# Seven block products instead of eight for three of eight k-tile pairs of the gate and up products

## The chip, the cores and the metric

The kernel runs on one core of a Trainium2 chip. The time is the device time of one execution in microseconds (us); a comparison takes the median of several runs. The profile is one execution taken by the hardware profiler. TensorE is called PE, with its weight loads apart as PEld, VectorE is DVE, ScalarE is ACT, GpSimd is POOL; SP is the queue that issues nearly all DMAs.

## The reference

One layer of a streaming encoder, 256 tokens of 2048 channels, all in float32:

```
x = x + 0.5 * swiglu(rms_norm(x, ffn1_norm), w_gate, w_up, w_down)
h = rms_norm(x, mix_norm);  proj = h @ w_in
x = x + concat([pool_mixer(u), gla_mixer(q, k, v, g, a)]) @ w_out
x = x + mem_cross_attention(rms_norm(x), rms_norm(mem), w_q, w_kv, w_o)
x = x + 0.5 * swiglu(rms_norm(x, ffn2_norm), w_gate, w_up, w_down)
out = rms_norm(x, final_norm)

def swiglu(h, w_gate, w_up, w_down):
    return (silu(h @ w_gate) * (h @ w_up)) @ w_down      # 2048 -> 5632 -> 2048
```

The change concerns `h @ w_gate` and `h @ w_up` in both feed-forward parts.

## The kernel before

**Numbers.** A float32 product is made of three products of float32r parts. An activation or a weight `a` is split into `hi` (a cast on ACT) and `lo = a - hi` (a subtraction on DVE); the product is `hi*hi + hi*lo + lo*hi`, three matmuls (`products`, L277). `xs` and `ys` hold activations already split, 16 k-tiles of 128 channels, each with hi and lo and 256 tokens, that is two halves of 128 tokens.

**Units.** All weights pass through one stream of units (`Stream`, L34). A unit is 1 MB of weights, 128 x 2048 float32. SP loads it into one of three `raw` buffers, ACT casts it into `wh` and DVE makes `wl` (three buffers each), and PE uses it. `emit` (L65) writes the program in this order: the split of unit u+2, the load of unit u+5, the matmuls of unit u. Work beside the stream (evictions, transposes, norms) is put in with `st.op(f, n)`: n units later. A scheduler at build time may still move instructions within an engine's list, but each engine then works its list strictly in order.

**Gate and up.** For 1024 output columns a `block_t` (L284) runs eight units over the 16 k-tiles, two k-tiles a unit. With two k-tiles, two column halves j and two token halves h a unit has eight block products of 128 x 128 by 128 x 512, 24 matmuls. They gather in two PSUM tiles of two banks each; PSUM holds four such tiles. The gate block is evicted by ACT (`ev_gate`, L463: Silu), the up block by DVE (`ev_up`, L468: times the gate), and the result is transposed by PE into `ys` (`turn`, L476: 16 transposes for a pair of blocks, then a cast and a subtraction for each half).

The loop (L486) goes over three parts of the 5632 columns: 4, 4 and 3 column blocks of 512. A part is two, two or one pairs of a gate and an up block (the third part ends with a block that holds 512 columns of both), and is followed by its down product (`into_x`, or `down_end` at the very end), whose units are plain ones too. A feed-forward part has 132 units; both have ten gate or up blocks of full width, five of each.

Of the kernel before, what the change touches and what calls it, by code (L numbers as in the profile page):

```python
# [33 lines left out]
class Stream:  # L34
# [23 lines left out]

    def unit(self, load, f, split=None):
        self.items.append((len(self.units), f))  # L60
        self.units.append((load, split))
        self.pending = [(n - 1, h) for n, h in self.pending]
        self._flush()

    def emit(self, load, split):  # L65
        done, w = -1, {}
# [12 lines left out]

def build(ctx, tc, I, out):  # L80
# [35 lines left out]
    def ctile():  # L116
        return tmp.tile([P, 2, S], F32, tag="c", name=uid("c"), bufs=2)

    def ttile():
        return tmp.tile([P, 2, S], F32, tag="t", name=uid("t"), bufs=3)  # L120

# [17 lines left out]


    ident = head.tile([P, 480], F32, tag="ident", name="ident")[:, :P]
    make_identity(nc, ident)
# [3 lines left out]
    for t in range(PAD):  # L146
        nc.gpsimd.memset(invc[:, t : t + 1], 1.0 / (t + 1))
    keep = const.tile([P, S], F32, tag="keep", name="keep")
    nc.gpsimd.memset(keep, 1.0)
    for c in range(S // CH):  # L150
        nc.gpsimd.memset(keep[:, c * CH : c * CH + 1], 0.0)
    gains = ctl("gains", [P, G_END])
    wa2 = const.tile([32, H * DK], F32, tag="wa2", name="wa2")
    R = const.tile([P, S], F32, tag="R", name="R")
    Rcol = ctl("Rcol", [P, 2])
# [36 lines left out]
    def diagonal(col):  # L192
        d = tmp.tile([P, P], F32, tag="diag", name=uid("diag"), bufs=4)
        nc.vector.tensor_scalar_mul(d, ident, col)
        return d
# [25 lines left out]

    diag = {}

# [7 lines left out]
    def spread_norm():  # L231

        ps = ptile(uid("ps"))
        for t in range(2):
            spread(ps[:, 0, :], t, diag["R"][t])
        nc.vector.tensor_copy(R, ps[:, 0, :S])

# [46 lines left out]
    def block_t(srcs, act, evict, delays=(0, 0)):  # L284
# [20 lines left out]
        for j in range(2):  # L305
            st.op(lambda j=j: evict(j, held["ps"][j]), delays[j])

    def block_b(srcs, act, evict, delay=0):
# [61 lines left out]

    rows = {}

# [37 lines left out]
    def more_gains():  # L410
        gain_columns(
            [("mix_norm", G_MIX, 16), ("xattn_norm", G_X, 16), ("mem_norm", G_MEM, 16),
             ("ffn2_norm", G_FFN2, 16), ("pool_scale", G_PS, 8), ("gla_head_norm", G_HN, 8),
             ("gla_b_a", G_BA, 4)], nc.sync,
        )
        for i in range(2):
            nc.sync.dma_start(wa2[16 * i : 16 * i + 16, :], I["gla_w_a2"][0])


# [26 lines left out]
    def into_x(w, act, scale, gain=None, k0=0, nk=KT, spread_too=True):  # L446

        for b in range(2):
            block_t(wwide(w, b * 2 * NB, k0, nk), act, residual(scale, b))
            if gain is not None:  # L450
                for j in range(2):
                    st.op(lambda c=2 * b + j: fold(c, gain), 1)
        if gain is not None:
            st.op(lambda: finish_norm(4, spread_too), 1)
            if spread_too:
                st.op(spread_norm, 2)

    FF_PARTS = ((0, 4), (4, 4), (8, 3))

    def ffn(wg, wu, wd, down):  # L460
        gate = {}

        def ev_gate(j, ps):  # L463
            g = gate[j] = scope["pool"].tile([P, 2, NB], F32, tag="sg", name=uid("sg"), bufs=4)
            for h in range(2):
                nc.scalar.activation(g[:, h, :], ps[:, h, :], AF.Silu, scale=Rcol[:, h : h + 1])  # L466

        def ev_up(j, ps):  # L468
            g = gate[j]
            for h in range(2):  # L470
                nc.vector.scalar_tensor_tensor(
                    out=g[:, h, :], in0=ps[:, h, :], scalar=Rcol[:, h : h + 1], in1=g[:, h, :],
                    op0=ALU.mult, op1=ALU.mult,
                )
# [11 lines left out]
        for lo, n in FF_PARTS:  # L486
            for b in range(0, n - 1, 2):
                n0 = (lo + b) * NB
                block_t(wwide(wg, n0), xs, ev_gate)
                block_t(wwide(wu, n0), xs, ev_up)  # L490
                for j in range(2):
                    st.op(lambda j=j, b=b: turn(gate[j], 4 * (b + j)), 1)
            if n % 2:
                def both(j, ps):
                    (ev_up if j else ev_gate)(0, ps)
                block_t(wtwo(wg, wu, (lo + n - 1) * NB), xs, both)
                st.op(lambda n=n: turn(gate[0], 4 * (n - 1)), 1)
# [11 lines left out]
    def down_first(wd, k0, nk, last):  # L509
        into_x(wd, ys, 0.5, G_MIX if last else None, k0, nk)  # L510

    ffn(I["ffn1_w_gate"][0], I["ffn1_w_up"][0], I["ffn1_w_down"][0], down_first)
    st.op(close_scope, 2)
    st.op(open_scope("s_mix"), 2)

# [4 lines left out]
    def mt(name, shape, tag=None, bufs=1):  # L520
        t = whole_lines(scope["pool"], shape, F32, tag or name, uid(name), bufs)
        mix[name] = t
        return t

    def m4():
# [8 lines left out]
    def ev_pool(b):  # L534
        def evict(p, ps):
# [4 lines left out]
            nc.gpsimd.memset(u[:, :, :PAD], 0.0)  # L540
            joined(ps, u[:, :, PAD:], R)
            src, dst, other, n = u, s0, s1, 1
# [62 lines left out]
    def ev_a():  # L605
# [4 lines left out]
        nc.vector.tensor_tensor(out=t, in0=ps[:32, 0, :S], in1=c[:32, 0, :], op=ALU.add)  # L610
        nc.vector.tensor_tensor(out=t, in0=t, in1=R[:32, :], op=ALU.mult)

    def decay():
        v = four(ptile(uid("pz")))
        for h in range(H):
            nc.tensor.matmul(
                v[:, h, :], wa2[:, h * DK : (h + 1) * DK], mix["aT"], start=True, stop=True
            )
# [9 lines left out]
        for h in range(H):  # L628
            nc.vector.tensor_tensor_scan(
                out=cum[:, h, :], data0=keep, data1=z[:, h, :], initial=0.0,  # L630
                op0=ALU.mult, op1=ALU.add,
# [9 lines left out]
        nc.scalar.activation(e, e, AF.Exp, scale=1.0 / 16)  # L641
        nc.gpsimd.tensor_tensor(out=e, in0=e, in1=bc(R, H), op=ALU.mult)
        mix["e"] = e
# [7 lines left out]
    def ev_q(p, ps):  # L651
        if p == 0:
# [3 lines left out]
        nc.vector.scalar_tensor_tensor(  # L656
            out=q, in0=q, scalar=DK ** -0.5, in1=bc(R), op0=ALU.mult, op1=ALU.mult
        )
# [101 lines left out]
    def ev_g(b):  # L760
        def evict(p, ps):
            h = 2 * b + p
            t = ttile()
            joined(ps, t, R)
            nc.scalar.activation(t, t, AF.Silu)
# [62 lines left out]
    def ev_Q(h):  # L828
        def evict(p, ps):
            t = ttile()  # L830
            joined(ps, t, R)
            split_pair(ys, 4 * h + 2 * p, t)
# [71 lines left out]
    into_x(w_o, ys, 1.0, G_FFN2, spread_too=False)  # L904
    st.op(close_scope, 2)
    st.op(open_scope("s_ffn2"), 2)

# [3 lines left out]
    def last_gain():  # L911
        fin["gB"] = scope["pool"].tile([P, D], F32, tag="gB", name="gB")
        nc.sync.dma_start(fin["gB"], I["final_norm"].partition_broadcast(P))
# [7 lines left out]
    def down_end(wd, k0, nk):  # L921
# [28 lines left out]
        def end_evict(nb, h):  # L950
            cols = slice(nb * NB, (nb + 1) * NB)
            if h == 0:
                fin[nb] = scope["pool"].tile([P, 2, NB], F32, tag="sg", name=uid("O"), bufs=4)
            xn, o = X[:, h, cols], fin[nb][:, h, :]
# [38 lines left out]

        st.op(ready_sqrt, 8)
        for b in range(2):
            for i, src in enumerate(wwide(wd, b * 2 * NB, k0, nk - 2)):
# [4 lines left out]

    st.op(last_gain, 20)
    ffn(I["ffn2_w_gate"][0], I["ffn2_w_up"][0], I["ffn2_w_down"][0], down_last)
    st.op(close_scope)


    raws = {}

# [4 lines left out]
    def split_unit(u, own):  # L1013
        raw = raws.pop(u)
        parts = [
            wpool.tile([P, 4 * NB], F32R, tag=t, name=f"{t}{u}", bufs=st.AHEAD + 1)
            for t in (("wh",) if own else ("wh", "wl"))
        ]
        if own:
            own(parts[0], raw)  # L1020
            return parts
# [5 lines left out]
        return hi, lo  # L1027

# [3 lines left out]
    for u in range(st.RAW):  # L1032
        load(u)
    st.emit(load, split_unit)

# [31 lines left out]
```

## Time and profile before

| | us |
|---|---|
| median of 3 runs | 2169.02 (2168.94 to 2169.61) |
| the profiled execution, its own time | 2167.38 |
| its span, first to last instruction | 2165.3 |
| PE busy in the span | 2147.6 (99%) |
| DVE busy | 1114.0 (51%) |
| ACT busy | 919.2 (42%) |
| mean granted TensorE clock | 0.998 |

A row of a group gives line, engine, operation, written and read tiles, shapes and count, then busy time and the mean duration of one in ns, then the engine's idle time ahead of them and who ended it. A row of a timeline gives the start in the span, the length, engine, line, tiles, the count of merged instructions and, in brackets, the idle time ahead of it. Matmuls are pipelined: one lasts longer than the distance to the next.

### The profile page before, as it was taken

To read this page: it belongs to the slowest core of one execution; us is meant where nothing else is said; L and a number is where in the kernel's file an instruction comes from. 1 tells how busy PE (TensorE), PEld (TensorE's weight loads), DVE (VectorE), ACT (ScalarE), POOL (GpSimd) and SP (SyncE) were. 2 spreads that over 40 slices of the span, in tenths; PEclk is the share of its full clock that TensorE was granted. 3 is DMA by queue.
4 is the path that set the end of the run, shared out by engine and by line. 5 is a ranking of instruction groups with operands and counts; after the bars stand their busy time and mean duration, and the time that the engine had idled before them with its cause. 6 is when DMAs were issued, how large, how long until landed. Compare 5 with 4: busy or idle time off the path is not lost.

```text
span 2165.3 us, 23828 instructions
## 1 busy us (share of the span) xinstructions
PE 2147.6 (99%) x10194; PEld 1798.8 (83%) x10194; DVE 1114.0 (51%) x847; ACT 919.2 (42%) x812; POOL 14.2 (1%) x41
## 2 busy tenths in 40 slices
PE   9999999999999999999999999999999999999998
PEld 7888888888888888888888888888888888888886
DVE  5444445445454677565565545554444444444544
ACT  6433333333333545455445444444433334333333
POOL 0000000000000000000000000000000000000001
PEclk9999999999999999999999999999999999999999
DMA  7555555555555555455555555555556555565553
GB/s 275 194 193 182 191 192 194 194 183 192 192 191 194 175 178 175 159 202 185 186 182 168 165 173 175 191 180 194 190 186 194 192 193 189 187 195 191 194 185 117
DMA packets 134674, 404.45 MB, mean 187 GB/s; under 512 B 8868, under 2 KB 12040, under 8 KB 134184
## 3 DMA queue, kind: packets, MB, share of 16 engines
q1 hardware_dynamic: 134536, 402.92, 56.0%
q8 instruction: 80, 1.31, 0.2%
q14 instruction: 26, 0.21, 0.0%
q10 hardware_dynamic: 32, 0.01, 0.0%
HBM read 400.80 MB, written 2.10 MB: 186 GB/s over the span
## 4 chain that ended last, share of the span: by engine, by line
PE 99%; DVE 1%; DMA 0%; issue 0%; ACT 0%; SPq 0%; DVEq 0%; ACTq 0%
PE pt L282 71%; PE pa L267 15%; PE pb L282 6%; PE pe L282 3%; PE ph L481 1%; PE pl L852 1%; PE pv L887 1%; PE px L434 0%; DMA X<-in_x 0%; PE px L400 0%; PE pa L600 0%; PE tm L814 0%; PE pq L709 0%; PE po L722 0%; PE ps L199 0%
## 5 line engine op out<-in xcount | busy, mean ns | idle before, releaser
L211 DVE TENSOR_TENSOR wl<-raw,wh 128x2048 fp32r<-128x2048 f32 (+2 forms) x382 | 865.1, 2265 | 974.5 <-ACT wh L210 974.4
L210 ACT CAST wh<-raw 128x2048 fp32r<-128x2048 f32 (+2 forms) x383 | 721.9, 1885 | 1076.6 <-PE pt L282 886.9
L282 PE MATMUL pt<-wh,xs 128*128 128x512 f32 x2816 | 871.7, 390 | 0.0
L282 PEld LDWEIGHTS pt<-wh,xs 128*128 128x128 f32 x2816 | 528.6, 188 | 109.7
L282 PE MATMUL pt<-wl,xs 128*128 128x512 f32 x1408 | 548.3, 389 | 0.0
L282 PE MATMUL pt<-wh,ys 128*128 128x512 f32 x1728 | 535.4, 389 | 0.0
L282 PEld LDWEIGHTS pt<-wh,ys 128*128 128x128 f32 x1728 | 324.4, 188 | 67.2
L282 PE MATMUL pt<-wl,ys 128*128 128x512 f32 x864 | 336.3, 389 | 0.0
L267 PE MATMUL pa<-xs,wh 128*128 128x512 f32 x896 | 317.6, 398 | 1.7 <-DVE t L241 1.7
L282 PEld LDWEIGHTS pt<-wl,xs 128*128 128x128 f32 x1408 | 264.5, 188 | 54.8 <-DVE wl L211 0.4
L267 PE MATMUL pa<-xs,wl 128*128 128x256 f32 x896 | 248.9, 281 | 0.0
L267 PEld LDWEIGHTS pa<-xs,wh 128*128 128x128 f32 x896 | 167.8, 188 | 41.0 <-issue 2.0
L282 PEld LDWEIGHTS pt<-wl,ys 128*128 128x128 f32 x864 | 162.2, 188 | 33.3
L267 PEld LDWEIGHTS pa<-xs,wl 128*128 128x128 f32 x896 | 169.2, 189 | 1.5 <-issue 0.2
L282 PE MATMUL pb<-wh,xs 128*128 128x512 f32 x384 | 121.7, 392 | 0.5 <-DVE ys L203 0.5
L282 PEld LDWEIGHTS pb<-wh,xs 128*128 128x128 f32 x384 | 72.0, 188 | 15.7 <-DVE ys L203 0.7
L282 PE MATMUL pb<-wl,xs 128*128 128x512 f32 x192 | 75.0, 391 | 0.0
L282 PE MATMUL pe<-wh,ys 128*128 128x512 f32 x192 | 59.4, 390 | 0.0
L282 PEld LDWEIGHTS pe<-wh,ys 128*128 128x128 f32 x192 | 36.0, 188 | 7.5
L282 PEld LDWEIGHTS pb<-wl,xs 128*128 128x128 f32 x192 | 36.1, 188 | 7.3 <-issue 0.2
L282 PE MATMUL pe<-wl,ys 128*128 128x512 f32 x96 | 37.5, 390 | 0.0
L466 ACT ACTIVATE sg<-pt,Rcol 128x512 f32<-128x512 f32 x44 | 27.9, 686 | 21.6 <-PE pt L282 21.5
(165 smaller groups left out, 687.9 us busy)
## 6 DMA issues: line engine op xcount, KB each, us to landing
raw<-in_ffn_w_down SPq DMA_DIRECT2D x88, 1024.0 KB, 5.1
raw<-in_ffn_w_up SPq DMA_DIRECT2D x80, 1024.0 KB, 5.0
raw<-in_ffn_w_gate SPq DMA_DIRECT2D x77, 1024.0 KB, 5.0
raw<-in_w_in SPq DMA_DIRECT2D x32, 1024.0 KB, 5.2
raw<-in_xattn_w_kv SPq DMA_DIRECT2D x32, 1024.0 KB, 5.3
raw<-in_w_out SPq DMA_DIRECT2D x16, 1024.0 KB, 5.3
raw<-in_xattn_w_q SPq DMA_DIRECT2D x16, 1024.0 KB, 5.0
raw<-in_xattn_w_o SPq DMA_DIRECT2D x16, 1024.0 KB, 5.3
```

Source lines behind the costliest of these rows:

```text
L210: nc.scalar.copy(hi, src)
L211: nc.vector.tensor_tensor(out=lo, in0=src, in1=f32(hi), op=ALU.subtract)
L267: nc.tensor.matmul(o, w, x, start=k == 0 and i == 0, stop=last and i == 1)
L282: nc.tensor.matmul(ps, a, w, start=first and i == 0, stop=last and i == 2)
L466: nc.scalar.activation(g[:, h, :], ps[:, h, :], AF.Silu, scale=Rcol[:, h : h + 1])
L481: nc.tensor.transpose(v[:, i, h * P : (h + 1) * P], g[:, h, i * P : (i + 1) * P], ident)
L852: nc.tensor.matmul(ps[:, t, :M], ys[:, 4 * h + d, a, tok], xa["K"][:, d, b, :], start=i == 0, stop=i == 11,)
L887: nc.tensor.matmul(ps[:, d, :S], xa["V"][:, m, a, col], xa["PT"][:, m, b, :], start=i == 0, stop=i == 5,)
```

## The change

Three of the eight units of a gate or up block, the k-tile pairs 0, 2 and 4, become S units. In an S unit the activations of the two k-tiles and two token halves are the four blocks of a 2 x 2 matrix, the weights of the two k-tiles and two column halves the blocks of another, and Strassen's identity (in Winograd's form) makes the four results of seven block products of sums. Each block product is still three matmuls, of sums that are split after they are made. The first gate block of each feed-forward part stays a `block_t`, as does the block of both; the other nine blocks are `block_s`.

The sums of activations (`part_sums`) are made once for each feed-forward part. The sums of weights are made for each S unit: `add_weights` makes four blocks (`T`, one buffer) with three DVE additions, `split_seven` splits `T` into the buffers `wh` and `wl`, and `rest` splits three blocks of `raw` itself into `xh` and `xl` (one buffer each). `emit` puts the additions one unit ahead of the split, and `rest` and the load behind it one unit later.

```
+            while done < min(u + ahead, len(self.units) - 1):
                 done += 1
-                w[done] = split(done, self.units[done][1])
-                if done + self.RAW < len(self.units):
-                    load(done + self.RAW)
+                while late:
+                    late.pop(0)()
+                if done + 1 < len(self.units):
+                    prepare(done + 1, self.units[done + 1][2])
+                w[done], rest = split(done, self.units[done][1])
...
+                def finish(done=done, rest=rest):
+                    if rest:
+                        rest()
+                    if done + self.RAW < len(self.units):
+                        load(done + self.RAW)
...
+                if rest:
+                    late.append(finish)
+                else:
+                    finish()
...
+    def add_weights(u, raw):
+        t = scope["pool"].tile([P, 4 * NB], F32, tag="T", name=f"T{u}")
+        w = raw.rearrange("p (b n) -> p b n", n=NB)
+        v = t.rearrange("p (b n) -> p b n", n=NB)
+        nc.vector.tensor_tensor(
+            out=v[:, 0:2], in0=w[:, 1:3], in1=w[:, 0:1].to_broadcast([P, 2, NB]), op=ALU.add
+        )
+        nc.vector.tensor_tensor(out=v[:, 2], in0=v[:, 0], in1=w[:, 2], op=ALU.add)
+        nc.vector.tensor_tensor(out=v[:, 3], in0=v[:, 2], in1=w[:, 3], op=ALU.add)
+        return t
+    def split_seven(u, raw, t):
...
+        split(th, tl, t)
+        def rest():
+            r = [scope["pool"].tile([P, 3 * NB], F32R, tag=n, name=f"{n}{u}") for n in ("xh", "xl")]
+            split(*r, raw[:, NB:])
...
+    def seven(banks, act, ext, i, g, first, later, weights):
+        th, tl, rh, rl = weights
...
+        table = {
+            "P1": (a11, rh[:, 0], rl[:, 0]), "P3": (n4, rh[:, 1], rl[:, 1]),
+            "P2": (a12, rh[:, 2], rl[:, 2]), "P5": (n1, th[:, 0], tl[:, 0]),
+            "P7": (s3, th[:, 1], tl[:, 1]), "P6": (s2, th[:, 2], tl[:, 2]),
+            "P4": (a22, th[:, 3], tl[:, 3]),
+        }
+        order = ("P1", "P7", "P5", "P6", "P2", "P3", "P4") if first else (
+            "P1", "P2", "P3", "P7", "P5", "P6", "P4")
+        for n in order:
+            (a, b), wh, wl = table[n]
+            for j, (x, w) in enumerate(((a, wh), (a, wl), (b, wh))):
+                nc.tensor.matmul(
+                    banks[n], x, w, start=first and j == 0,
+                    stop=not later and n in ("P1", "P5", "P6", "P7") and j == 2,
+                )
```

A `block_s` holds all four PSUM tiles, a, b, c and d. P1, P6, P7 and P5 have the banks of a and b, P2 and P4 those of c, P3 one of d; the plain units add into c and d. After the third S unit `combine` reads a and b, and at the end of the block `join` adds its result to c (j = 1) and d (j = 0), ahead of the eviction, which now reads SBUF:

```
+        def combine():
+            e = held["e"] = scope["pool"].tile([P, 4, NB], F32, tag="sg", name=uid("sg"), bufs=2)
+            a, b = held["parts"]
+            nc.scalar.copy(e[:, 0], a[:, 0])
+            nc.vector.tensor_tensor(out=e[:, 3], in0=a[:, 1], in1=e[:, 0], op=ALU.add)
+            nc.vector.tensor_tensor(
+                out=e[:, 1:3], in0=b, in1=e[:, 3:4].to_broadcast([P, 2, NB]), op=ALU.add
+            )
+            nc.vector.tensor_tensor(out=e[:, 3], in0=b[:, 1], in1=e[:, 1], op=ALU.add)
+        def join(j):
+            e = held["e"][:, 0:2] if j else held["e"][:, 2:4]
+            nc.vector.tensor_tensor(
+                out=e, in0=held["ps"][j], in1=e, op=ALU.add if j else ALU.subtract
+            )
+            evict(j, e)
...
+                if lo == b == 0:
+                    block_t(wwide(wg, n0), xs, lambda j, ps: ev_gate(j, ps, 1))
+                else:
+                    block_s(wwide(wg, n0), xs, Ext(), PAIRS, lambda j, c: ev_gate(j, c, 0))
+                block_s(wwide(wu, n0), xs, Ext(), PAIRS, ev_up)
...
+                wait = PAIRS[-1] + 2 if b + 2 < n - 1 else 1
                 for j in range(2):
-                    st.op(lambda j=j, b=b: turn(gate[j], 4 * (b + j)), 1)
+                    st.op(lambda j=j, b=b, held=held: turn(held[j], 4 * (b + j)), wait)
```

The transposes of a pair that is followed by another pair in the same part so move from one unit behind the pair to six units behind it, into the next gate block. `keep`, `wa2` and `R` move into the pools of the stages that use them, `gB` (the final gain) takes the buffer of `T` and is loaded two units into the last down product and not twenty units into the second feed-forward part, and `finish_norm`, `spread_norm` and the change of a stage's pool shift by one unit.

More of the change, by code (lines that the diff above doesn't have):

```diff
@@ L57, in op, with unit, emit @@
         self._flush()
-    def unit(self, load, f, split=None):
+    def unit(self, load, f, split=None, prepare=None):
         self.items.append((len(self.units), f))
-        self.units.append((load, split))
+        self.units.append((load, split, prepare))
         self.pending = [(n - 1, h) for n, h in self.pending]
         self._flush()
-    def emit(self, load, split):
-        done, w = -1, {}
+    def emit(self, load, prepare, split):
+        done, w, late = -1, {}, []
         for u, f in self.items:
@@ L137, in ctl @@
         return whole_lines(const, shape, F32, name, name)
-    ident = head.tile([P, 480], F32, tag="ident", name="ident")[:, :P]
+    ident = head.tile([P, P], F32, tag="ident", name="ident")
     make_identity(nc, ident)
@@ L235, in spread_norm @@
             spread(ps[:, 0, :], t, diag["R"][t])
+        R = rows["R"] = scope["pool"].tile([P, S], F32, tag="R", name=uid("R"))
         nc.vector.tensor_copy(R, ps[:, 0, :S])
@@ L306, in block_t, with part_sums @@
             st.op(lambda j=j: evict(j, held["ps"][j]), delays[j])
+    def part_sums(act, ext, i, g):
+        t = scope["pool"].tile([P, 4 * NB], F32, tag="T", name=uid("T"))
+        a = t[:, :NB].rearrange("p (k s) -> p k s", k=2)
+        e = t[:, NB : 2 * NB].rearrange("p (n s) -> p n s", n=4)
+        nc.vector.tensor_tensor(
+            out=a, in0=f32(act[:, 2 * g : 2 * g + 2, 0, :]), in1=f32(act[:, 2 * g : 2 * g + 2, 1, :]),
+            op=ALU.add,
+        )
+        a11, a21, a12, a22 = (a[:, k, h * P : (h + 1) * P] for k in range(2) for h in range(2))
+        nc.vector.tensor_tensor(out=e[:, 3], in0=a11, in1=a21, op=ALU.subtract)
+        nc.vector.tensor_tensor(out=e[:, 1], in0=a22, in1=a21, op=ALU.subtract)
+        nc.vector.scalar_tensor_tensor(
+            out=e[:, 2], in0=e[:, 1], scalar=-1.0, in1=a11, op0=ALU.mult, op1=ALU.subtract
+        )
+        nc.vector.tensor_tensor(out=e[:, 0], in0=a12, in1=e[:, 2], op=ALU.add)
+        split(ext[:, i, 0], ext[:, i, 1], e)
@@ L453, in into_x, with pair_sums, f, __getitem__ @@
         if gain is not None:
-            st.op(lambda: finish_norm(4, spread_too), 1)
+            st.op(lambda: finish_norm(4, spread_too), 2)
             if spread_too:
-                st.op(spread_norm, 2)
+                st.op(spread_norm, 3)
     FF_PARTS = ((0, 4), (4, 4), (8, 3))
+    PAIRS = (0, 2, 4)
+    def pair_sums(g, delay):
+        def f():
+            if g == PAIRS[0]:
+                rows["xe"] = scope["pool"].tile(
+                    [P, len(PAIRS), 2, 4, P], F32R, tag="xe", name=uid("xe")
+                )
+            part_sums(xs, rows["xe"], PAIRS.index(g), g)
+        st.op(f, delay)
+    class Ext:
+        def __getitem__(self, i):
+            return rows["xe"][i]
     def ffn(wg, wu, wd, down):
         gate = {}
-        def ev_gate(j, ps):
-            g = gate[j] = scope["pool"].tile([P, 2, NB], F32, tag="sg", name=uid("sg"), bufs=4)
+        def hidden():
+            e = scope["pool"].tile([P, 4, NB], F32, tag="sg", name=uid("sg"), bufs=2)
+            return {0: e[:, 2:4], 1: e[:, 0:2]}
+        def ev_gate(j, c, fresh):
+            if fresh and fresh == 1 + j:
+                gate["new"] = hidden()
+            g = gate["new"][j] if fresh else c
+            gate[j] = g
             for h in range(2):
-                nc.scalar.activation(g[:, h, :], ps[:, h, :], AF.Silu, scale=Rcol[:, h : h + 1])
-        def ev_up(j, ps):
+                nc.scalar.activation(g[:, h, :], c[:, h, :], AF.Silu, scale=Rcol[:, h : h + 1])
+        def ev_up(j, c):
             g = gate[j]
@@ L523, in mt, with mixer_constants @@
         return t
+    def mixer_constants():
+        keep = mt("keep", [P, S])
+        nc.gpsimd.memset(keep, 1.0)
+        for c in range(S // CH):
+            nc.gpsimd.memset(keep[:, c * CH : c * CH + 1], 0.0)
+        wa2 = mt("wa2", [32, H * DK])
+        for i in range(2):
+            nc.sync.dma_start(wa2[16 * i : 16 * i + 16, :], I["gla_w_a2"][0])
+    st.op(mixer_constants, 2)
     def m4():
@@ L641, in decay @@
         nc.scalar.activation(e, e, AF.Exp, scale=1.0 / 16)
-        nc.gpsimd.tensor_tensor(out=e, in0=e, in1=bc(R, H), op=ALU.mult)
+        nc.gpsimd.tensor_tensor(out=e, in0=e, in1=bc(rows["R"], H), op=ALU.mult)
         mix["e"] = e
@@ L656, in ev_q @@
         nc.vector.scalar_tensor_tensor(
-            out=q, in0=q, scalar=DK ** -0.5, in1=bc(R), op0=ALU.mult, op1=ALU.mult
+            out=q, in0=q, scalar=DK ** -0.5, in1=bc(rows["R"]), op0=ALU.mult, op1=ALU.mult
         )
@@ L994, in down_end @@
         st.op(ready_sqrt, 8)
+        st.op(last_gain, 2)
         for b in range(2):
@@ L1014, in split_unit @@
         raw = raws.pop(u)
+        if own is split_seven:
+            return split_seven(u, raw, summed.pop(u))
         parts = [
```

120 lines of the change are left out of this document (85 added, 35 removed).

## The prediction

> **What bounds the kernel now.** I read the page's head first, then its chain that ended last, then its costliest groups.
>
> ```profile
> span 2165.3 us, 23828 instructions
> PE 2147.6 (99%) x10194; PEld 1798.8 (83%) x10194; DVE 1114.0 (51%) x847; ACT 919.2 (42%) x812; POOL 14.2 (1%) x41
> PE 99%; DVE 1%; DMA 0%; issue 0%; ACT 0%; SPq 0%; DVEq 0%; ACTq 0%
> L211 DVE TENSOR_TENSOR wl<-raw,wh 128x2048 fp32r<-128x2048 f32 (+2 forms) x382 | 865.1, 2265 | 974.5 <-ACT wh L210 974.4
> L210 ACT CAST wh<-raw 128x2048 fp32r<-128x2048 f32 (+2 forms) x383 | 721.9, 1885 | 1076.6 <-PE pt L282 886.9
> ```
>
> PE is both the busiest engine and 99% of the chain: matmuls alone set the time. DVE idles for ACT's cast, and ACT for PE to free a buffer, so the splits run at PE's pace with room to spare. How much room is in the gate and up stage itself: first a row of the chain in order of time (start, length, piece), then one of a gate and an up block by windows (busy PE, PEld, DVE, ACT).
>
> ```profile
> 458.46 174.10 PE pt L282 x768
> 369.65:456.71 87.06, 87.06 (x387) 72.03 (x386) 41.59 (x22) 33.14 (x22) 0.00 (x0) 1.00 0.55 188
> ```
>
> 768 matmuls without a gap in 174.10 us are m = 0.2267 us each, so a unit of 24 is 5.44 us. In the pair's 87.06 us PE never pauses, and DVE works 41.59, ACT 33.14.
>
> **What is removed.** The lists of the two built programs hold 10138 and 9976 matmuls and transposes: 162 fewer, 3 for each of 3 S units in 18 blocks, all 128x512 ones. 162 x 0.2267 = 36.7 us, all of it on the path, so the floor is 2169.0 - 36.7 = 2132.3 us. An S unit lasts 21m = 4.76 us.
>
> **What is added on DVE and ACT.** The rows by shape:
>
> ```profile
> L211 DVE TENSOR_TENSOR wl<-raw,wh 128x2048 fp32r<-128x2048 f32 x374 | 857.4, 2293 | 970.1 <-ACT wh L210 970.0
> L211 DVE TENSOR_TENSOR wl<-raw,wh 128x1024 fp32r<-128x1024 f32 x4 | 4.9, 1224 | 1.6 <-ACT wh L210 1.6
> L211 DVE TENSOR_TENSOR wl<-raw,wh 128x512 fp32r<-128x512 f32 x4 | 2.8, 692 | 2.8 <-ACT wh L210 2.8
> L210 ACT CAST wh<-raw 128x2048 fp32r<-128x2048 f32 x374 | 714.9, 1911 | 1068.9 <-PE pt L282 886.9 <-PE pa L267 76.2 <-issue 40.4
> L210 ACT CAST ys<-t 128x512 fp32r<-128x512 f32 x12 | 7.4, 619 | 1.2 <-DVE t L243 0.7 <-DVE t L767 0.5
> L466 ACT ACTIVATE sg<-pt,Rcol 128x512 f32<-128x512 f32 x44 | 27.9, 686 | 21.6 <-PE pt L282 21.5
> ```
>
> 128x1536 lies on the lines between: 1.76 us on DVE, 1.48 on ACT. How closely they follow each other is in the timeline of DVE, and once of ACT and PE (start, length):
>
> ```profile
> 183.15 2.29 DVE L211 TENSOR_TENSOR wl<-raw,wh 128x2048 fp32r<-128x2048 f32 x1 [3.15 <-ACT wh L210]
> 185.35 2.72 DVE L471 SCALAR_TENSOR_TENSOR sg<-pt,Rcol,sg 128x512 f32<-128x512 f32 x4
> 194.02 2.29 DVE L211 TENSOR_TENSOR wl<-raw,wh 128x2048 fp32r<-128x2048 f32 x1 [3.14 <-ACT wh L210]
> 196.23 2.35 DVE L211 TENSOR_TENSOR ys<-ph,ys 128x1024 fp32r<-128x1024 f32 x2
> 746.55 0.16 DVE L188 TENSOR_TENSOR chain<-chain,Rcol 128x2 f32<-128x2 f32 x1
> 746.75 0.16 DVE L189 TENSOR_TENSOR chain<-chain 128x2 f32<-128x2 f32 x1
> 192.08 1.90 ACT L210 CAST wh<-raw 128x2048 fp32r<-128x2048 f32 x1 [3.53 <-PE pt L282]
> 2095.39 0.93 PE L481 MATMUL ph<-ident,sg 128*128 128x128 f32 x7
> ```
>
> The four of L471 start at 185.35, 0.09 ahead of 183.15 + 2.29: independent instructions overlap by 0.09, so 2048 elements cost 2.20, 1536 1.67, 1024 1.13, 512 0.60. One that reads its forerunner's result starts 0.04 after that ends (746.55 + 0.16 to 746.75); so does DVE after ACT (192.08 + 1.90 to 194.02). Seven transposes last 0.93 to the end of the last; I take 0.85 for what eight hold PE.
>
> An S unit thus gives DVE three additions (1.13 + 0.60 + 0.60, some 0.3 more as they depend on each other) and `rest` (1.67) on top of its split: 4.3 more. A block adds `combine` (1.13 + 2 x 0.60) and two joins (2 x 1.13), 4.6. For a pair of S blocks DVE goes from 41.6 to 41.6 + 6 x 4.3 + 2 x 4.6 = 76.6 us, PE from 87.1 to 83.0: 92%. ACT goes to 33.1 + 6 x 1.48 + 2 x 0.6 = 43.2. DVE still fits on average, but its list is in strict order and `xh`, `xl`, `T` have one buffer, so what counts is when a split arrives.
>
> The place to look is `xl` of a block's second S unit, u+2 (u is the block's first unit). PE frees `xh` of unit u at P3, which stands late, and needs the new `xl` 21 to 25 matmuls on. I walked the lists of the built program through this place with the durations above. For an up block behind a gate block that carried the previous pair's transposes (four blocks: the second pair of parts one and two, in each feed-forward part) the lists are
>
> ```
> DVE  join(c) wl(u) wl(u+1) ys join(d) T(u+2) x3 wl(u+2) wl(u+3) T(u+4) first xl(u+2)
> ACT  silu x4 wh(u+2) wh(u+3) xh(u+2)
> PE   u: 12 | 6 of P2, P4 | half of u+1: 12 | P3: 3 | other half: 12 | u+2: 6 of P7, P5 | 3 | xl needed
> ```
>
> Zero is the start of unit u-1 on PE. DVE has nothing it may do until bank c is complete, at 12m = 2.72. Then: join 3.9, wl(u) 6.1, wl(u+1) 8.3, the subtraction of the second transposes 9.45, join 10.6, three additions 13.2; ACT casts wh(u+2) 13.25 to 15.15; wl(u+2) 17.4, wl(u+3) 19.6, first addition 20.7, xl(u+2) 22.5. PE: unit u-1 with eight transposes ends at 6.3, 12 matmuls 9.05, P2 waits for the bank the transposes held until 9.5 (0.45 late), 33 more 17.0, the wait for wl(u+2) 0.3, 8 more 19.3, then idle to 22.5: 3.2. Sum 3.9 us a block, 15.6 for four (in part one the additions and the second join stand in another order, at the same price).
>
> In the 14 other blocks the same walk finds `xl` in time. First S block behind plain units (6; zero at the last plain unit): wh(u+3) is cast once P4 is done, 9.55 to 11.45, wl(u+3) 13.7, last addition 14.3, xl 16.0; needed 17.7. Up block behind a gate block without transposes (4): join 5.5, join 7.3, two Silus and the cast 8.7, wl(u+2) 10.95, addition 12.1, wl(u+3) 14.3, addition 14.9, xl 16.6; needed 17.7. Gate block behind an up block (4): joins 7.6, `ev_up` and additions 11.6, cast 13.5, wl 15.75, xl 17.5; needed 17.7, only 0.2 to spare. I add 1.5 us for slips there and for PE's restart after a wait, between 0 and 14 x 1.1 = 15 (every margin but the widest missed by its own size).
>
> Costed at nothing: `part_sums` (by the same lines 7.5 us of DVE and 1.9 of ACT for each feed-forward part, in the plain `block_t`, where DVE idles 3.15 of 5.44 us; without that cover 19 us in all). The SP queue carries as many raw loads as before, each tied to a DVE release; one lands 5.0 us after issue and is wanted over 10 us after its buffer is free. `gB` and `wa2` only change their place in that queue; `R`, the norms and the pool changes are units ahead of their readers.
>
> ```profile
> raw<-in_ffn_w_up SPq DMA_DIRECT2D x80, 1024.0 KB, 5.0
> gB<-in_final_norm SPq DMA_DIRECT2D x1, 1024.0 KB, 4.7
> ```
>
> Sum: -36.7 + 15.6 + 1.5 = -19.6. The profiled execution (2167.4, its span 2165.3 and 2.1 around it) would become 2147.8; the median of the runs shown lies 1.6 above it: 2149.4, say 2149 us.
>
> [...]
>
> **The rivals.** *DVE becomes the bound.* The lists put T, cast and wl behind each other at the head of DVE's list, and each such step idles DVE for the cast, 1.95 us. Six of them in a pair of blocks make 76.6 + 11.7 = 88.3 us against PE's 83.0, and PE would wait 2.65 a block in all 18: 2169.0 - 36.7 + 47.7 = 2180. It decides from 36.7 / 18 = 2.04 us a block on. For it: 92%, one buffer each, and margins down to 0.2. Against: units 5 to 7 of each block are plain and leave DVE over 3 us each to catch up.
>
> *The waits are hidden.* If the four late blocks find DVE ahead of my walk (the join for bank c ready earlier, the additions overlapping), most of 15.6 returns: about 2134. For it: the late step hangs on one order of four instructions. Against: that order is fixed, and `wl(u+3)` and an addition stand ahead of `xl(u+2)` in it.
>
> *The clock falls in the waits.* At the end of the span PE has stopped and the granted clock (the eighth figure here, after the stretch, its length and five engines) falls:
>
> ```profile
> 2156.00:2160.00 4.00, 0.00 (x0) 0.00 (x0) 2.67 (x9) 1.91 (x7) 1.40 (x2) 0.74 0.68 262
> 2160.00:2165.30 5.30, 0.00 (x0) 0.00 (x0) 1.20 (x3) 0.36 (x1) 0.00 (x0) 0.50 0.51 198
> ```
>
> 0.74 over 4 us is half clock after about 1.9. A wait of 3.2 could trip that; if it took as long as those 4 us to come back, at half speed, each of four blocks would lose 2 us: 2157. [...]
>
> That the change does not do what it says is excluded by the count of matmuls.
>
> **How the numbers follow.** My forecast (2142 to 2156) 0.53, hidden waits 0.18, the clock 0.05, DVE as the bound 0.24, of which a third ends near break-even. About 0.2% (4.3 us) can be told from no change. Faster: 0.53 + 0.18 + 0.05 = 0.76; within it 0.08; slower 0.16. The range runs from the hidden case, 2136, to two thirds of the way from break-even to the DVE case's price, 2173, and leaves out about 0.05 below and 0.12 above.
>
> **What would show it.** PE at 9976 or so matmuls, DVE near 1114 + 54 x 4.3 + 18 x 4.6 + 15 = 1444 us busy, ACT near 919 + 54 x 1.48 + 18 x 0.6 + 4 = 1014. In the waits of PE, `xl` should lead, with four of about 3.2 us, all in second S units of up blocks behind transposes, then `wl` and a PSUM bank with 0.3 to 0.5. Many `xl` or `wl` waits of 1 us and more in the other 14 blocks would prove the walk wrong, as would PE waiting for raw loads or a granted clock under 0.98.

## The result and the profile after

| | before | after |
|---|---|---|
| median | 2169.04 us (2168.94 to 2169.61, 4 runs) | 2156.01 us (2155.12 to 2157.21, 4 runs) |
| ratio | | 0.9940, 95% interval 0.9923 to 0.9957 |
| the profiled execution, its own time | 2167.38 | 2156.07 |
| its span | 2165.3 | 2154.2 |
| matmuls and transposes on record | 10194 | 10032 |

The change makes the kernel 13.0 us faster; the forecast was 20, at 2149. The 162 matmuls are gone to the last one, so 36.7 us were saved and some 24 lost again. First the head of the page after the change, the chain that ended last by engine, and two rows of its groups:

```profile
span 2154.2 us, 23983 instructions
PE 2122.0 (99%) x10032; PEld 1771.5 (82%) x10032; DVE 1428.1 (66%) x1189; ACT 1007.4 (47%) x890; POOL 14.1 (1%) x41
PE 92%; DVE 5%; issue 2%; ACT 1%; DMA 1%; SPq 0%; DVEq 0%; ACTq 0%
L217 DVE TENSOR_TENSOR xl<-raw,xh 128x1536 fp32r<-128x1536 f32 x54 | 94.6, 1753 | 4.0 <-ACT xh L216 3.7
L216 ACT CAST xh<-raw 128x1536 fp32r<-128x1536 f32 x54 | 80.0, 1482 | 52.5 <-PE pt L383 22.1
```

PE is still 99% busy, but the chain now runs through DVE for 5%: there are places where the end of a subtraction decides. (The share alone is no measure of a loss: the fastest kernel below shows 5% too.) PE's busy time fell by 2147.6 - 2122.0 = 25.6 us only, 11 less than the matmuls taken out; the rest of the loss is idle time. The view of PE's waits (what waited and for whom, us in total, times, longest) finds the idle part:

```profile
PE pt L383 <- DVE xl L217: 10.7, 5, 2.9
PE pgain L521 <- DMA gain<-in_ffn_norm: 4.1, 1, 4.1
PE pt L383 <- DVE ys L217: 3.6, 4, 2.1
PE pa L274 <- DVE t L248: 1.7, 1, 1.7
```

10.7 us for `xl`, 3.6 for a PSUM bank that the transposes' subtraction holds. The other two rows stand at places that the change did not touch. All long waits for `xl` and for the bank lie in the four up blocks behind transposes. This is the block whose first unit is 72, by the timeline of DVE (start, length):

```profile
397.74 1.22 DVE L434 TENSOR_TENSOR sg<-pt,sg 128x1024 f32<-128x1024 f32 x1 [3.17 <-PE pt L289]
398.88 2.28 DVE L217 TENSOR_TENSOR wl<-T,wh 128x2048 fp32r<-128x2048 f32 x1
401.08 2.28 DVE L217 TENSOR_TENSOR wl<-raw,wh 128x2048 fp32r<-128x2048 f32 x1
403.28 1.22 DVE L217 TENSOR_TENSOR ys<-ph,ys 128x1024 fp32r<-128x1024 f32 x1
...
410.27 2.29 DVE L217 TENSOR_TENSOR wl<-T,wh 128x2048 fp32r<-128x2048 f32 x1 [2.06 <-ACT wh L216]
412.48 2.28 DVE L217 TENSOR_TENSOR wl<-raw,wh 128x2048 fp32r<-128x2048 f32 x1
414.68 1.22 DVE L345 TENSOR_TENSOR T<-raw 128x1024 f32<-128x1024 f32 x1
415.81 1.75 DVE L217 TENSOR_TENSOR xl<-raw,xh 128x1536 fp32r<-128x1536 f32 x1
```

DVE idles 3.17 us, then works without a hole up to the cast for `wl(u+2)`, and `wl(u+3)` and an addition stand ahead of `xl(u+2)`, as the prediction's list has it. On PE this place looks so, by its timeline, followed by the same stretch by windows (busy PE, PEld, DVE, ACT, POOL, granted clock, DMA share, GB/s):

```profile
414.33 0.39 PE L383 MATMUL pt<-xh,xe 128*128 128x512 f32 x1
417.62 0.53 PE L383 MATMUL pt<-xl,xs 128*128 128x512 f32 x1 [2.90 <-DVE xl L217]
417.96 0.61 PE L383 MATMUL pt<-xh,xs 128*128 128x512 f32 x1
418.37 0.63 PE L383 MATMUL pt<-xl,xs 128*128 128x512 f32 x1
418.79 0.63 PE L383 MATMUL pt<-xh,xs 128*128 128x512 f32 x1
...
421.35 0.41 PE L383 MATMUL pt<-wh,xs 128*128 128x512 f32 x1
```

```profile
414.50:417.60 3.10, 0.22 (x1) 0.00 (x0) 3.10 (x4) 0.00 (x0) 0.00 (x0) 1.00 0.54 137
417.60:420.00 2.40, 2.38 (x6) 1.95 (x7) 1.26 (x2) 1.00 (x1) 0.00 (x0) 0.58 0.98 367
420.00:422.00 2.00, 2.00 (x7) 1.57 (x6) 1.07 (x1) 2.00 (x2) 0.00 (x0) 0.66 0.95 391
422.00:426.00 4.00, 4.00 (x19) 3.30 (x19) 4.00 (x3) 2.17 (x2) 0.00 (x0) 1.00 0.04 8
```

A wait of 2.90 us, and behind it the matmuls start 0.41 to 0.43 apart and not 0.2267, with a granted clock of 0.58 and 0.66. From 417.96 to 421.35 eight matmuls take 3.39 us in place of 1.81: 1.58 us lost while PE counts as busy. So about half of the missing 11 us of PE time is half clock behind waits. Most of the rest is counted as busy without being work: the last matmul before each wait lasts 0.39 us, 0.16 more than the distance to the next, and the first one behind a wait holds up the next by 0.11.

Summed over all S blocks as the distance between the starts of successive matmuls less 0.2267, the losses of this execution are:

| place | us |
|---|---|
| blocks 72, 270, 318: bank 0.67, `wl` 0.20, `xl` 3.05 (means) | 3.95 + 3.91 + 3.92 = 11.8 |
| the same blocks: half clock | 1.58 + 1.60 + 1.58 = 4.8 |
| the same blocks: restart after a wait, nine times 0.11 | 1.0 |
| block 24: bank 2.27, `xl` 1.92, restarts 0.22, no half clock | 4.4 |
| four gate blocks behind up blocks: short waits for `xl`, once for `wl` too, with restarts | 0.31 + 0.77 + 0.31 + 0.31 = 1.7 |

These are 23.7 of the 36.7 - 11.1 = 25.6 us that the span does not show. 0.85 more, net, lie between the two feed-forward parts, where the same waits as before are followed by half clock in this execution; 1.1 are spread thinly. These rows are the stretch behind those waits, of before and of after:

```profile
926.00:930.00 4.00, 3.91 (x22) 3.48 (x23) 3.90 (x9) 1.56 (x4) 0.00 (x0) 1.00 0.82 261
```

```profile
919.00:922.00 3.00, 2.82 (x10) 2.42 (x11) 2.90 (x7) 0.87 (x3) 0.00 (x0) 0.62 0.86 223
```

### The profile page after: what moved, and what is told of

The parts are those of the page before. It is cut to its first block, busy times and chain, and to the rows that moved or that the text cites. A ratio compares the mean times of both kernels' runs of the same rounds, so it can differ in the third digit from the quotient of the medians.

```text
span 2154.2 us, 23983 instructions
## 1 busy us (share of the span) xinstructions
PE 2122.0 (99%) x10032; PEld 1771.5 (82%) x10032; DVE 1428.1 (66%) x1189; ACT 1007.4 (47%) x890; POOL 14.1 (1%) x41
## 4 chain that ended last, share of the span: by engine, by line
PE 92%; DVE 5%; issue 2%; ACT 1%; DMA 1%; SPq 0%; DVEq 0%; ACTq 0%
PE pt L289 54%; PE pa L274 15%; PE pt L383 10%; PE pb L289 6%; PE pe L289 3%; DVE wl L217 2%; ACT wh L216 1%; PE ph L643 1%; DVE xl L217 1%; DVE T L345 1%; PE pl L1036 1%; PE pv L1071 1%; PE px L571 0%; DVE sg L434 0%; DMA raw<-in_ffn_w_gate 0%
## 5 line engine op out<-in xcount | busy, mean ns | idle before, releaser
L217 DVE TENSOR_TENSOR wl<-raw,wh 128x2048 fp32r<-128x2048 f32 (+2 forms) x328 | 740.2, 2258 | 530.9 <-ACT wh L216 529.9
L216 ACT CAST wh<-raw 128x2048 fp32r<-128x2048 f32 (+2 forms) x329 | 618.4, 1881 | 671.7 <-PE pt L289 471.4
L289 PE MATMUL pt<-wh,xs 128*128 128x512 f32 x1952 | 616.6, 390 | 0.0
L289 PEld LDWEIGHTS pt<-wh,xs 128*128 128x128 f32 x1952 | 366.6, 188 | 76.0
L289 PE MATMUL pt<-wl,xs 128*128 128x512 f32 x976 | 380.6, 390 | 0.0
L289 PEld LDWEIGHTS pt<-wl,xs 128*128 128x128 f32 x976 | 183.6, 188 | 37.7
L216 ACT CAST wh<-T 128x2048 fp32r<-128x2048 f32 x54 | 103.1, 1909 | 190.0 <-DVE T L349 148.6
L217 DVE TENSOR_TENSOR wl<-T,wh 128x2048 fp32r<-128x2048 f32 x54 | 123.8, 2292 | 88.9 <-ACT wh L216 88.9
L383 PE MATMUL pt<-wh,xe 128*128 128x512 f32 x324 | 114.5, 394 | 2.1 <-DVE ys L217 2.1
L217 DVE TENSOR_TENSOR xl<-raw,xh 128x1536 fp32r<-128x1536 f32 x54 | 94.6, 1753 | 4.0 <-ACT xh L216 3.7
L289 PEld LDWEIGHTS pb<-wh,xs 128*128 128x128 f32 x384 | 72.1, 188 | 15.6 <-DVE ys L209 0.7
```

What stands on the lines that cost most here:

```text
L216: nc.scalar.copy(hi, src)
L217: nc.vector.tensor_tensor(out=lo, in0=src, in1=f32(hi), op=ALU.subtract)
L289: nc.tensor.matmul(ps, a, w, start=first and i == 0, stop=last and i == 2)
L383: nc.tensor.matmul(banks[n], x, w, start=first and j == 0, stop=not later and n in ("P1", "P5", "P6", "P7") and j == 2,)
```

## The experiments

The theory under test: the losses sit in four places, are made by the order of DVE's list there (DVE has the time), and half clock comes from PE's pause. The main rival: DVE is short of time as a whole, so that a wait which is taken away comes back elsewhere.

### One split ahead of another

```
-                while late:
-                    late.pop(0)()
+                    while late:
+                        xl = late.pop(0)()
+                        if done - 1 in (26, 74, 272, 320):
+                            order.enter_context(self.tc.issue_after(xl.ins))
```

What is written next in the program, the addition for u+4 and the split of u+3, queues behind `xl(u+2)` on DVE.

> Theory (the wait for xl is DVE's order, and the half clock comes from the wait): the split of xl of the second S unit (units 26, 74, 272, 320) is issued on DVE right behind wl of the same unit, ahead of the next unit's first addition and wl. In the run with the change these four waits cost 1.9, 3.1, 3.0 and 3.1 us, and the three longer ones are followed by 1.4 to 1.6 us of matmuls at half clock. xl would end 3.4 us earlier, at the moment PE wants it; the next wl is wanted some 0.2 us before it is there. Sum -11.1 - 4.5 - 0.4 (restarts) + 0.8 = -15, so 2141 us, and no granted clock near 0.6 in these blocks. Rival (DVE is short of time as a whole): the waits move on to wl of unit u+3 or to the next S unit at about the same price, 2152 to 2158. Rival (half clock has another source than the wait): 2145 to 2147 with half clock still there.

Measured: 2143.41 us (2143.07 to 2144.96, 4 runs), 12.6 less than the change for one instruction moved past two in four places. The waits of PE:

```profile
PE pt L388 <- DVE ys L221: 3.7, 4, 2.1
PE pt L388 <- DVE xl L221: 2.4, 5, 0.6
```

The bank waits are as before, those for `xl` fell from 10.7 to 2.4, and no half clock is left in these blocks. 2.4 us of the expected 15 are missing. The timeline of DVE in block 72 says why:

```profile
410.38 2.29 DVE L221 TENSOR_TENSOR wl<-T,wh 128x2048 fp32r<-128x2048 f32 x1 [2.05 <-ACT wh L220]
413.56 1.76 DVE L221 TENSOR_TENSOR xl<-raw,xh 128x1536 fp32r<-128x1536 f32 x1 [0.89 <-ACT xh L220]
```

`xl` could start at 412.6, but the cast `xh` still stood behind `wh(u+3)` on ACT, which costs it 0.89 us and PE a wait of 0.53. The rival of a DVE short of time is out for these blocks: the work is the same, and the waits did not come back.

### Matmuls on zeros in the wait

```
+        if fill:
+            order = ("P7", "P5", "P1", "P2", "P3", "P6", "P4")
...
+                if fill and n == "P5":
+                    for _ in range(fill):
+                        mm = nc.tensor.matmul(banks["P5"], zero, th[:, 0], start=False, stop=False)
+                    queue.enter_context(tc.issue_after(mm.ins))
```

> The order on DVE stays late, but in the second S unit of three late blocks (units 74, 272, 320) PE gets 13 more matmuls, of a stationary tile of zeros, into the bank of P5, issued between P5 and P1. They add nothing to the result and take 13 x 0.2267 = 2.95 us, inside the wait of 3.05. Theory (PE's pause halves the clock): the pause becomes 0.1 us, no half clock follows, and the time falls by 1.5 to 1.6 us in each of the three blocks: 2151.3 us, though 39 matmuls more run. Rival (slow matmuls come from what is read, the fresh xl and xh, or from traffic beside them): unchanged, 2156, or slower. Rival (more work on PE is simply longer): 2156 + 39 x 0.2267 = 2165.

Measured: 2153.23 us (2152.08 to 2154.72, 4 runs): 39 useless matmuls more, and 2.8 us less. The same stretch of block 72 by windows:

```profile
414.40:416.80 2.40, 2.40 (x13) 1.97 (x11) 2.40 (x2) 0.00 (x0) 0.00 (x0) 1.00 0.56 118
416.80:419.00 2.20, 2.20 (x10) 1.57 (x9) 1.57 (x3) 0.48 (x1) 0.00 (x0) 1.00 1.09 402
419.00:421.00 2.00, 2.00 (x11) 1.65 (x10) 0.54 (x1) 2.00 (x2) 0.00 (x0) 1.00 0.96 379
```

The clock stays at 1.00, with the same splits and the same transfers beside it: the half clock of after came from PE's pause, not from traffic or from fresh operands. It is gone in all three blocks. The profiled execution, the fastest of the four with 2152.08, saves 4.0 of the expected 4.7 us; what the other three lost besides is not on record. In block 24, which had no half clock in the execution of after, there is some here, behind a bank wait of the same 2.1 us. It holds PE up by 1.6 us and costs nothing in the end, because the wait for `xl` behind it falls from 1.92 to 0.28: PE only comes later to what it waits for.

> As with 13 matmuls on zeros in three late blocks, but 5 of them: 1.13 us of the wait of 3.05 filled, so that PE pauses 1.9 us. Theory (half clock needs a pause of over 2 us): no half clock behind these three pauses, and a time like that with 13, 2152 to 2153. Rival (a shorter pause does it too, by where it falls): half clock behind some of the three, 1.5 us each, 2153.5 to 2156.

Measured, one run: 2153.72 us. This is above the 2152 to 2153 of the theory, and no more than one execution of a kernel whose executions differ by 2 to 3 us, so the trace has to decide. The waits of PE for `xl`:

```profile
PE pt L388 <- DVE xl L219: 8.4, 8, 1.8
```

PE paused 1.8 us in the three blocks, and but for the restart matmuls went on 0.2267 apart behind each of them. So a pause of 1.8 spared the clock three times of three, and one of 2.9 cost it three times of three; that of 2.1 in block 24 cost it in one execution and not in three others.

The traces show what separates those. In the execution of after the granted clock is 0.50 in four stretches ahead of the end of the span, from 417.96, 919.72, 1568.26 and 1831.08 us on. By windows, the first of them with the stretch ahead of it and the one behind it, then the other three:

```profile
414.55:417.96 3.41, 0.51 (x2) 0.30 (x2) 3.41 (x4) 0.00 (x0) 0.00 (x0) 1.00 0.60 171
417.96:421.37 3.41, 3.41 (x10) 2.67 (x9) 1.33 (x3) 2.37 (x2) 0.00 (x0) 0.50 0.99 382
421.38:424.79 3.41, 3.41 (x17) 2.83 (x16) 3.41 (x2) 2.79 (x2) 0.00 (x0) 1.00 0.15 61
919.72:923.13 3.41, 3.41 (x13) 2.82 (x12) 3.31 (x8) 1.56 (x3) 0.00 (x0) 0.50 0.80 277
1568.26:1571.67 3.41, 3.41 (x10) 2.64 (x9) 1.37 (x2) 2.88 (x2) 0.00 (x0) 0.50 0.98 354
1831.08:1834.49 3.41, 3.41 (x9) 2.63 (x8) 1.37 (x2) 2.79 (x2) 0.00 (x0) 0.50 1.00 366
```

Each lasts 3.41 us, and the distances of their starts, 501.76, 648.54 and 262.82 us, are 147, 190 and 77 times 3.413; no other length near 3.41 divides all three. In the other traces too every stretch of half clock starts a whole number of these lengths after the one before it, and lasts one of them or two. So the span can be divided into windows of 3.413 us. Divided this way, the waits of block 24 look so, first with the zeros, then after the change, by windows:

```profile
140.89:144.31 3.42, 1.43 (x6) 1.21 (x7) 3.42 (x4) 0.32 (x1) 0.00 (x0) 1.00 0.73 242
144.31:147.72 3.41, 3.41 (x9) 2.64 (x9) 2.07 (x3) 2.21 (x3) 0.00 (x0) 0.50 0.17 67
```

```profile
138.07:141.48 3.41, 2.62 (x12) 1.83 (x10) 3.41 (x3) 1.25 (x2) 0.00 (x0) 1.00 0.00 0
141.48:144.89 3.41, 2.09 (x9) 1.74 (x10) 3.41 (x4) 0.98 (x2) 0.00 (x0) 1.00 0.90 308
144.89:148.31 3.42, 3.42 (x17) 2.83 (x16) 1.41 (x3) 2.23 (x3) 0.00 (x0) 1.00 0.01 2
```

With the zeros PE idles 1.99 us in one window, and the next is at half clock throughout; after the change the same pause is divided into 0.79 and 1.32, and no window is at half clock. In the feed-forward parts of all ten kernels' traces, the start of the span aside, each of the 11 windows in which PE idled 1.97 us or more was followed by half clock, and none of those with 1.94 or less; in the trace of after these are three with 2.57, 2.66 and 2.90, and the largest of the others has 1.32.

### The four late blocks made plain

```
-                block_s(wwide(wu, n0), xs, Ext(), PAIRS, ev_up)
+                if b == 2:
+                    block_t(wwide(wu, n0), xs, ev_up)
+                else:
+                    block_s(wwide(wu, n0), xs, Ext(), PAIRS, ev_up)
```

> The up block of the second pair of parts one and two in each feed-forward part (the four late blocks) is made of plain units again, 24 matmuls each; all else stays. Theory (the cost sits in these four blocks): it gives back 4 x 9 x 0.2267 = 8.2 us of matmuls and ends the losses there, 4.5 + 6.0 + 6.0 + 6.0 = 22.5 us, 2156.0 + 8.2 - 22.5 = 2141.7 us, with perhaps 1 to 3 us of the waits left at the second transposes. So four S blocks fewer would be faster than all 18. Rival (DVE behind as a whole): the other 14 blocks become late or stay so and the time is 2156 or above.

Measured: 2143.18 us (2142.79 to 2144.22, 4 runs), near the 2141.7 worked out; PE still waits 1.7 us for `xl`, in other blocks. With 14 S blocks the kernel is 12.8 us faster than with 18. The cost sat in these four.

### Nothing but what was moved

```
-                if lo == b == 0:
-                    block_t(wwide(wg, n0), xs, lambda j, ps: ev_gate(j, ps, 1))
-                else:
-                    block_s(wwide(wg, n0), xs, Ext(), PAIRS, lambda j, c: ev_gate(j, c, 0))
-                block_s(wwide(wu, n0), xs, Ext(), PAIRS, ev_up)
+                block_t(wwide(wg, n0), xs, lambda j, ps: ev_gate(j, ps, 1))
+                block_t(wwide(wu, n0), xs, ev_up)
...
-                wait = PAIRS[-1] + 2 if b + 2 < n - 1 else 1
+                wait = 1
```

> All 18 blocks are plain (24 matmuls a unit), with the transposes one unit on as before the change; what is left of the change is the sums of the activations (part_sums), the moves of R, gB, wa2, c, t and the diagonals into scoped pools, and the new queue of loads. Theory (the moved parts cost nothing): 2169 us within 1.5. Rival (the moves take part of the gain): 2172 to 2178, of which the difference to 2169 is their price.

Measured: 2168.36 us (2166.67 to 2168.77, 10 runs), ratio 0.9996, interval 0.9986 to 1.0005. The sums of the activations and all moves of buffers cost nothing that can be told from noise, and the floor of the change is 2168.36 - 36.73 = 2131.6 us, good to about 1 us.

### Other S units

Only the line `PAIRS = (0, 2, 4)` is changed, to `(0, 4)` and to `(0, 3, 6)`.

> Two S units a block, its units 0 and 4, in place of three. 54 - 18 = 36 S units save 108 matmuls, 24.5 us, so the floor is 2144.6. Theory (the loss is a place, not the number of S units): unit 4 has three plain units ahead of it, xl is there in time, and only the bank waits at the transposes are left, 0.8 to 2.4 us in four blocks: 2146 to 2152 us, less loss than with three. Rival (every S unit costs DVE its share of PE's time): the loss of 24 us falls by a third to 16, 2160 us.

Measured: 2142.69 us (2142.43 to 2143.15, 4 runs), better than the 2146 to 2152 worked out: less 24.5 us of matmuls from 2168.4 would be 2143.9. The view of PE's waits shows none in an S block, not at the transposes either, where the theory still had some. As the change stands, its third S unit saves 12.2 us of matmuls and costs 2156.0 - 2142.7 + 12.2 = 25.5.

> The three S units of a block are its units 0, 3 and 6 in place of 0, 2 and 4; all else as the change has it, so the transposes go to the end of the block. Theory: xl(u+3) has one unit, 5.4 us, more and its waits go; but combine, both joins and both sets of transposes now meet at the block's end, and P2 of the next block waits for the second transposes' bank: some 7.4 us after the last plain unit by the order of DVE's list, where PE is there after 4.2, so 3.2 us in four blocks, with half clock behind it in some. 2132.3 + 4 x (3.3 to 4.9) + 2 = 2148 to 2154 us. Rival (distance is all that matters): 2133 to 2137.

Measured: 2173.13 us (2168.92 to 2175.67), 10 runs, ratio 1.0018, interval 1.0008 to 1.0027, so a shade slower than before the change; both values worked out were wrong. The theory had the right mechanism and looked for it at the wrong bank. The waits of PE, and DVE's timeline in the gap between the blocks at 16 and 24:

```profile
PE pt L383 <- DVE sg L434: 18.5, 12, 3.9
PE pt L383 <- DVE sg L430: 4.0, 2, 2.0
PE pt L383 <- DVE ys L217: 2.1, 1, 2.1
```

```profile
139.31 1.23 DVE L345 TENSOR_TENSOR T<-raw 128x1024 f32<-128x1024 f32 x1 [0.23 <-DMA raw<-in_ffn_w_up]
140.45 2.29 DVE L217 TENSOR_TENSOR wl<-raw,wh 128x2048 fp32r<-128x2048 f32 x1
142.66 2.35 DVE L434 TENSOR_TENSOR sg<-pt,sg 128x1024 f32<-128x1024 f32 x2
```

`xl` is out of the list, as both theories said. But with `combine` one unit before the end, the two joins (L434) release the banks in which the next block begins, at its first product and not only at P2, and they stand behind an addition and a split. Twelve such waits cost 18.5 us. Half clock follows five of all the waits in the feed-forward parts, the three longest, of 3.4 to 3.9, and two of 2.0 to 2.1 (for the other two rows), but neither one of 2.0 nor one of 2.3 that falls into two windows of 3.413 us. The matmuls and DVE's work are those of the change (DVE 1430.1 us busy, after 1428.1), and the time differs by 17 us: where DVE's work falls decides, not how much it is.

### The order at four places

To `xl` ahead of `wl(u+3)` come `xh(u+2)` ahead of `wh(u+3)` on ACT, `wl(u)` ahead of the join for bank c, and the second transposes' subtraction ahead of `wl(u+1)`, in the same four blocks:

```
+                        if done - 3 in self.LATE:
+                            for ins in hi_lo:
+                                order.enter_context(self.tc.issue_after(ins))
+                    if done - 1 in self.LATE:
+                        order.enter_context(self.tc.issue_after(self.turned))
...
+        def join_behind():
+            with tc.issue_after(st.first_lo[after]):
+                join(1)
```

> In the four late blocks (first units u = 24, 72, 270, 318) the order is set at four places: wl(u) is issued on DVE ahead of the join for bank c, the second transposes' subtraction ys ahead of wl(u+1), xl(u+2) ahead of the addition for u+4 and wl(u+3), and on ACT xh(u+2) ahead of wh(u+3). In the run with xl alone moved, each of the blocks at 72, 270 and 318 still lost 0.66 us at the bank and 0.68 at xl, each with 0.11 of restart, and the block at 24 lost 2.27 + 0.11 at the bank. Theory (only the order is late, DVE has the time: it idled 3.2 us ahead of the join for c): all of these go, 3 x 1.56 + 2.38 = 7.1 us, less some 1 to 2 that stay, so 2143.4 - 5.5 = 2138 us. Rival (DVE has no time left): wl(u+1) and the second join come later and PE waits there, 2142 to 2146.

Measured: 2135.05 us (2133.66 to 2137.07, 4 runs), ratio to before 0.9843, interval 0.9828 to 0.9858, 3 us better than the 2138 worked out. It beats both kernels. The waits of PE and DVE's timeline in block 72:

```profile
PE pt L392 <- DVE xl L224: 0.8, 1, 0.8
PE pt L297 <- DVE wl L224: 0.3, 1, 0.3
```

```profile
392.10 2.29 DVE L224 TENSOR_TENSOR wl<-T,wh 128x2048 fp32r<-128x2048 f32 x1 [2.03 <-ACT wh L223]
394.31 1.22 DVE L443 TENSOR_TENSOR sg<-pt,sg 128x1024 f32<-128x1024 f32 x1
395.44 1.22 DVE L224 TENSOR_TENSOR ys<-ph,ys 128x1024 fp32r<-128x1024 f32 x1
...
404.50 2.29 DVE L224 TENSOR_TENSOR wl<-T,wh 128x2048 fp32r<-128x2048 f32 x1 [2.05 <-ACT wh L223]
406.71 1.75 DVE L224 TENSOR_TENSOR xl<-raw,xh 128x1536 fp32r<-128x1536 f32 x1
```

The 3.17 us that DVE idled ahead of the join are down to 2.03, ahead of `wl(u)`, which now fills part of that time. `xl(u+2)` follows its `wl` at once and starts 12.4 us after that join, where it was 18.1. 3.4 us are left above the floor of 2131.6. DVE at 67% of the span is enough for three S units a block.

## Why the prediction was right, and which of its terms was too small

The sign, the place and the mechanism were right; 2156.0 lies inside the range and 7 us above the forecast.

**Removed: right.** 162 matmuls fewer on record (both traces count 56 more than the lists did), and the S units run at the 0.2267 us of the plain ones wherever PE neither waits nor has half clock. The run with the moves alone puts the floor at 2131.6 (forecast 2132.3).

**Added on DVE and ACT: right.** DVE 1428.1 us busy (forecast 1444), ACT 1007.4 (1014).

**The walk: right to 0.2 us.** With its zero 2.72 us before the join for bank c, at 395.02, the steps of block 72 end, forecast and measured: wl(u) 6.1 and 6.1, wl(u+1) 8.3 and 8.3, the subtraction of the transposes 9.45 and 9.5, wl(u+2) 17.4 and 17.5, wl(u+3) 19.6 and 19.7, the addition 20.7 and 20.9, xl(u+2) 22.5 and 22.5. In the blocks at 72, 270 and 318 the three waits are on average 0.67, 0.20 and 3.05 us (forecast 0.45, 0.3, 3.2). Together with the block at 24 that is 16.0 us against 15.6, but at 24 the agreement is luck. DVE's list has an addition ahead of the transposes' subtraction there, which ends 10.6 us from zero and not 9.45, so that the bank costs 2.27 where 0.45 was forecast and `xl` 1.92 where it was 3.2. `xl` starts 1.13 after the addition of 1.22 (414.68 to 415.81) and `wl(u+2)` is followed after 2.21, not 2.29, so overlap of 0.08 to 0.09 is there, as the row of before had it.

**The 1.5 us for slips and restarts: half of what came.** The slips in the 14 other blocks were 1.7 with their restarts, all in four gate blocks behind up blocks, which the walk had with 0.2 to spare and which came 0.2 to 0.4 late. The restarts in the late blocks, 1.2 more, were not covered.

**What failed: the price of a late block ended with its waits.** 3.9 us each were summed, and the clock behind the wait was made a rival of its own at 0.05. It belonged into the sum: half clock for 3.4 us, 1.6 lost, in three of the four blocks, 4.8 in all; restarts of 0.11 after each wait add 1.2, and half clock behind an older wait 0.85, net. The zeros in the wait show that the pause is the cause, since the clock stays at 1.00 with them. The rival's 2 us a block and its total of 2157 were close. The row from the end of the span (half clock after about 1.9 us of rest) was in hand, and the prediction gave it too little weight: in these runs 2.9 us sufficed each time, and 2.0 us where they fell within one window of 3.413 us.

**DVE as the bound: wrong as priced, possible in another place.** The runs with the order changed lost the waits without a change in DVE's work. The spacing 0, 3, 6 came to 2173, near the 2180 of this rival, with the same work: there it took a crowd at the banks, not 92% of DVE.

**The hidden waits: not by themselves.** 2134 was priced for a DVE ahead of the walk; 2135 is what the kernel reaches when four instructions are put in the right order.

**The range.** Two thirds of the way from 2169 to 2180 would be 2176; the 2173 of the prediction is one third. Its lower end, 2136, stands above the hidden case's 2134. The measured time is far from both ends.

## What to carry to other kernels

When a saving on the bounding engine is paid with work on another that has time on average, walk the second engine's list at the places where evictions, transposes and splits meet: there the order of three or four instructions decides; setting it by hand brought 21 us, more than the change had brought without it. Price a wait of PE with what follows it: a pause of 2.9 us cost 4.5 here, one of 1.8 little beyond itself. And try fewer of the change: two S units a block gave 13 us more than three, until the order was mended.

## What the runs showed of the hardware

A pause of PE of 2.9 us was followed by 3.4 us at half clock (matmuls 0.424 apart in place of 0.2267) three times of three; one of 2.1 once in four executions of the same block; 1.8 never in three. What separates them is where the pause falls: half clock (granted 0.50) came and went in steps of 3.413 us, after the change at starts 147, 190 and 77 of them apart, and in the feed-forward parts, the start of the span aside, it followed each of the 11 windows of that length with 1.97 us or more of PE's idle time and none with 1.94 or less.

Outside the feed-forward parts less sufficed. A pause of 1.65 us, 2 us behind one of 1.0, was followed by half clock in the five executions in which it fell within one window, and not in the five in which a window's end divided it. After the change it lay from 917.53 to 919.18, and half clock began at 919.72; before the change, with windows counted back from the half clock that begins at 2157.95, it lay from 924.44 to 926.09 and a window ended at about 925.8. Many of the matmuls around it are smaller; why less suffices there is not shown.

With matmuls whose stationary operand is all zeros in the waits of three blocks, 13 in each, the granted clock stayed at 1.00 there (0.58 and 0.66 without them), and the kernel was 2.8 us faster with these 39 matmuls than without.
